# Block 0's product 4 one level deeper, its result added in memory by accumulating transfers

## The chip, the cores and the metric

One core of one Trainium2 chip. The metric is device time in microseconds of one execution, as the median of several runs. The runs of one kernel on one chip spread over 0.3 to 1.7 us, mostly under 1.1, and the median of the same kernel moves by up to 0.8 us between chips, so times are compared below between kernels that ran in turn on the same chip. (Profiles of different runs are also laid side by side; their chips can differ.)

## The reference

```python
x: (16, 512, 768)  w1: (768, 3072)  b1: (3072,)  w2: (3072, 768)      # float32

def reference(x, w1, b1, w2):
    y = np.matmul(x, w1) + b1
    y = 0.5 * y * (1.0 + erf(y / np.sqrt(2.0)))       # exact GELU
    return np.matmul(y, w2).astype(np.float32)
```

The 8192 rows are worked in eight blocks of 1024. Both products are done by Strassen-Winograd: seven products of half-size operands in place of eight. In the second product of blocks 2 to 7, each of the seven is split once more in the same way ("nested level"). Blocks 0 and 1 are mixed: most of their second product runs one level deep in row units, a few of the seven products run nested.

## The kernel before

What the change and the argument touch. A row unit of block 0 or 1 takes 128 rows and runs the products with 384 columns on the moving side; `mm` skips the products that a nested level does for it:

```python
class Unit2:                       # one-level unit: 128 rows, N2 = 384 columns, NH = 12 chunks
    def mm(self, p, dst, first, c0, c1):
        if p == 2 or self.lean and p in (1, 4):      # lean: block 1
            return
        ...
        for c in range(c0, c1):
            nc.tensor.matmul(out=dst[:, 0:N2], lhsT=a, rhs=w[:, :, c, :], ...)

    def left_done(self, row, bank):
        if row == 0:
            if not self.lean:                        # partial sum of block 0 kept for product 2
                nc.scalar.copy(out=self.rows(par02), in_=bank[:, 0:N2])
            return
        ...
```

A nested level does one of the seven products for all four row units at once, by seven sub-products of 6 chunks and 2 row halves, 192 columns each:

```python
HYBRID = ((0, 2), (1, 1), (1, 4), (1, 2))            # (block, product)

class UnitH(Unit3):
    def mm(self, q, dst, first, c0, c1):
        for c in range(NQ):                          # NQ = 6
            for t in range(2):
                nc.tensor.matmul(out=dst[:, t * N4:(t + 1) * N4], lhsT=a,     # N4 = 192
                                 rhs=self.w[q][:, c, :], ...)
    def finish(self):
        if self.p == 2:
            for n in range(NU):
                nc.gpsimd.dma_start(out=orr[...], in_=self.dst[:, n // 2, n % 2])
```

Everything is software-pipelined in periods: the matmuls of one unit are interleaved with those of the unit before, and between them "slots" put vector work and transfers in their queues. The very end of the kernel matters later: the last product of block 7 is finished in two halves, and its results leave by a few last stores:

```python
def last(self, banks):
    for t in range(2):
        self.mm(4, banks[t], True, 0, self.C, (t,))
        o = self.dst[:, 1, t, 0, :]
        tt(o, banks[t][:, t * N4:(t + 1) * N4], o, ADD)
        (nc.sync, nc.scalar)[t].dma_start(out=orr[...], in_=o)      # the last stores of the kernel
```

Of the kernel before, what the change touches and what calls it, by code (L numbers as in the profile page):

```python
# [8 lines left out]
FP32 = mybir.dt.float32  # L9
F16 = mybir.dt.float16  # L10
P = 128
ADD = mybir.AluOpType.add
# [10 lines left out]
def kernel(  # L23
# [128 lines left out]
    tmps1 = [tmp_at(o_tmp + 4 * k * RH) for k in range(2)]  # L152
    o_stage = o_wt + 2 * N + PAR
    stage = [cut(o_stage + k * WB, WB, "p (c n) -> p c n", c=NQ)
# [6 lines left out]
    for slot, off in ((T2, o_x0), (T1, o_x0 + W2_N + 2 * GS_N), (T4, o_x1 + XT_N)):  # L161
        w2v[slot] = cut(off, W2_N, "p (h c n) -> p h c n", h=2, c=NH)
    GS = [cut(o, GS_N, "p (c r) -> p c r", c=NH)
          for o in (o_x0 + W2_N, o_x0 + W2_N + GS_N, o_x1, o_x1 + GS_N)]
    osbs = [[cut(o, n).bitcast(FP32) for o, n in zip(oo, (2 * N2, 2 * N))]
            for oo in ((o_x1 + 2 * GS_N + 2 * N + 2 * N2, o_wt),
                       (o_x1 + 2 * GS_N + 2 * N, o_x1 + 2 * GS_N))]
    assert 2 * N + 4 * N2 <= PAR
    par02, par1, par4 = [cut(o, PAR).bitcast(FP32).rearrange(
        "p (r t h n) -> p r t h n", r=2, t=2, h=2) for o in (o_wt + 2 * N, 2 * XT_N, o_x1 + 2 * GS_N)]  # L170
    par11 = cut(o_w2, W2P).bitcast(FP32).rearrange("p (c n) -> p c n", c=NH)[:, 0:8, 0:N4].rearrange(
# [7 lines left out]
    def wb_at(off):  # L179
        return cut(off, WB, "p (c n) -> p c n", c=NQ)  # L180

    hyb_lev = [[strip(0, 0, 0, 0), strip(1, 1, 0, 0), Gs[0][1][:, 0:NQ, 0, 2 * P:RH], strip(1, 1, NQ, 0)],
               [strip(0, 1, 0, 0), strip(0, 0, NQ, 0), strip(0, 1, NQ, 0), strip(0, 0, 0, 2 * P)],
               [strip(0, 1, 0, 2 * P), strip(0, 0, NQ, 2 * P), strip(0, 1, NQ, 2 * P), strip(0, 0, 0, 0)],
               [strip(0, 1, 0, 0), strip(0, 0, NQ, 0), strip(0, 1, NQ, 0), strip(0, 0, NQ, 2 * P)]]
    spare = stage + [wb_at(2 * XT_N + o) for o in
                     (PAR, PAR + WB, XT_N, XT_N + WB)]
    xh_mid = [cut(2 * XT_N + XT_N + 2 * WB + k * K, K) for k in (2, 3, 4, 0, 1)]
    assert XT_N + 2 * WB + 5 * K == GR // 2
    hyb_w = {2: {7: stage[0], 5: stage[1], 6: stage[2], 4: stage[5]},  # L190
             1: dict(zip((7, 4, 5, 6), map(wb_at, (o_x0 + W2_N, o_x0 + W2_N + WB, o_x1, o_x1 + WB)))),
             4: {7: wb_at(o_x1), 4: wb_at(o_x1 + WB), 5: stage[3], 6: stage[4]}}

# [9 lines left out]
    with tc.manual_schedule():  # L203
# [63 lines left out]

        def split_w2(p, t, q=None):

            b11, b12, b21, b22 = quarters(p)  # L270

            def put(q, src, eng=nc.sync):
                eng.dma_start(out=w2s[p, q][:], in_=src)

            t = {n: spare[k] for n, k in zip((7, 5, 6, 4), t)}
            for n, a, b in ((7, b22, b12), (5, b12, b11), (6, b22, t[5]), (4, b21, t[6])):
                def f(n=n, a=a, b=b):
                    tt(t[n], a, b, SUB)
                    puts.append([LAG[0], lambda eng: put(n, t[n], eng)])
                later(WB, f, slow if q is None else q)  # L280

        def load_w2s(p, qs):
            for q in qs:
                nc.sync.dma_start(out=hyb_w[p][q], in_=w2s[p, q][:])

# [72 lines left out]

        HYBRID = ((0, 2), (1, 1), (1, 4), (1, 2))

        def operand(sb, p):
            return OPERAND[p] if sb else Gs[0][1][:, :, 0, :]

# [71 lines left out]
        class Unit2:  # L435
# [4 lines left out]
            def __init__(self, g, sb, u):  # L440
                self.g, self.sb, self.u = g, sb, u
                self.lean = sb > 0
                self.eng = nc.gpsimd if self.lean else nc.sync
                self.o = osbs1[u - NU] if self.lean else osbs[u % 2]

            def mm(self, p, dst, first, c0, c1):
                if p == 2 or self.lean and p in (1, 4):
                    return
                r = slice(self.u * P, (self.u + 1) * P)
                G1, G2 = g_of(self.sb)  # L450
                w = w2v[SLOT[p]]
                for c in range(c0, c1):
                    a = {1: G1[:, c, 0, r], 4: G2[:, c, 1, r],
                         3: GS[3][:, c, :], 5: GS[0][:, c, :], 6: GS[1][:, c, :],
                         7: GS[2][:, c, :]}[p]
                    nc.tensor.matmul(out=dst[:, 0:N2], lhsT=a, rhs=w[:, :, c, :],  # L456
                                     start=first and c == 0, stop=c == self.C - 1,
                                     skip_group_check=True)
# [7 lines left out]
            def c12(self):  # L466
                return self.o[0]

# [3 lines left out]
            def right_done(self):  # L472
                self.eng.dma_start(out=orr[:, self.sb * 8 + self.u, N2:N], in_=self.o[0])

            def left_done(self, row, bank):
                if row == 0:
                    if not self.lean:
                        nc.scalar.copy(out=self.rows(par02), in_=bank[:, 0:N2])
                    return
                if self.lean:  # L480
                    tt(self.o[1][:, 0:N2], bank[:, 0:N2], self.rows(par4), ADD)
                else:
                    nc.scalar.copy(out=self.o[1][:, 0:N2], in_=bank[:, 0:N2])
                self.eng.dma_start(out=orr[:, self.sb * 8 + NU + self.u, :], in_=self.o[1])

# [97 lines left out]
        class UnitH(Unit3):  # L583

            def __init__(self, g, sb, m):
                self.g, (self.sb, self.p) = g, HYBRID[m]
                self.lev, self.w = hyb_lev[m], dict(hyb_w[self.p])
                b11, _, b21, b22 = quarters(self.p)
                self.w.update({1: b11, 2: b21, 3: b22})
                self.add = {0: par02, 1: par1}[self.sb] if self.p == 2 else None  # L590
                self.dst = {1: par1, 4: par4, 2: par11}[self.p] if self.sb else par02
                self.alloc = lambda: None
# [15 lines left out]
            def finish(self):  # L608
                if self.p == 2:
                    for n in range(NU):  # L610
                        nc.gpsimd.dma_start(
                            out=orr[:, self.sb * 8 + n, 0:N2].rearrange("p (h n) -> p h n", h=2),
                            in_=self.dst[:, n // 2, n % 2])

# [332 lines left out]

        def drain(slot, eng=nc.sync, wait=True):
            for f in puts:
                f[0] -= 1  # L950
            while puts and not (wait and puts[0][0] > 0):
                puts.pop(0)[1](eng)
            if slot > 1:
                for f in raws[:2]:
                    f()
                del raws[:2]

        def fill_mm2_one(sb, U, slot):
            if slot == 1:
                flush(queue)  # L960
                g_sum(2, U, q=soon)
                if U == 0:
                    g_sum(3, U, q=soon)
                flush(soon)
                if U == 0:
                    for p in (1, 2, 3, 5, 6, 7, 4):
                        raw_w2(p)
                    for p, t in ((6, (0, 1, 2, 3)), (1, (4, 5, 0, 1)), (4, (2, 3, 4, 5)), (2, (0, 1, 2, 5))):
                        split_w2(p, t)
            drain(slot)  # L970
            if slot == 2:
# [10 lines left out]
            if U + 1 == NU and slot == 4:  # L982
                lev_sums(None, m=0, ks=(2,))
            if U + 1 == NU and slot == 2:
                lev_sums(None, m=1, ks=(0, 1, 2))
            if slot > 1:
# [9 lines left out]
        def fill_hyb(sb, m, slot):  # L996
            drain(slot)
            if m == 0 and slot == 1:
                load_w2s(1, (7, 4))
                lev_sums(None, m=1, ks=(3,))  # L1000
            if m == 0 and slot == 4:
                load_w2s(1, (5, 6))
            if m == 0 and slot == 5:
                lev_sums(None, m=2)
            if m == 1 and slot == 5:
                lev_sums(None, m=3, ks=(0, 1))
            if m == 1 and slot == 6:
                split_w2(7, (6, 7, 8, 9))
                split_w2(5, (6, 7, 8, 9))
            if (m, slot) in ((1, 6), (2, 1), (2, 3), (2, 5), (3, 1), (3, 5)):  # L1010
                slow.pop(0)[1]()
            if m == 2 and slot == 1:
                load_w2s(4, (7, 4))
                lev_sums(None, m=3, ks=(2,))
            if m == 2 and slot == 5:
                lev_sums(None, m=3, ks=(3,))
            if m == 3 and slot == 2:
                for k in (0, 1):
                    g_sum(k, NU)
            if slot > 0:  # L1020
                sums(1200)
            if slot == 6:
                flush(queue)
                if m == 1:
                    load_next_x(2, range(5))
                if m == 3:
                    for t in range(3):
# [5 lines left out]
        def fill_lean(sb, k, slot):  # L1033
# [12 lines left out]
            if k == 0 and slot == 4:  # L1046
                LAG[0] = 3
                split_w2(3, (1, 2, 3, 4))
            if slot > 1:
# [114 lines left out]
```

## Time and profile before

| | before |
|---|---|
| time, median of 6 runs | 852.17 us (851.51 to 852.36) |
| span in the profile | 850.3 us |
| tensor engine (PE) busy | 843.9 us |
| its instructions in the program | 12949 |
| block 0's second product, first matmul to block 2's first | 120.53 to 224.33 us |
| start of the last matmul to the end of the span ("tail") | 4.03 us |

PE is the bound: the lines in the prediction below show it. Three more lines of the PE timeline of the kernel before give the marks that I compare with later: the first matmul of the stage, the first of block 2, and the last group of the kernel. Columns: start in us, duration, engine, line, what it writes and reads, form, count.

```profile
120.53 2.11 PE L456 MATMUL bX<-arena 128*128 128x384 f16 x12
...
224.33 0.81 PE L411 MATMUL bX<-arena 128*128 128x512 f16 x3
...
845.40 1.15 PE L516 MATMUL bX<-arena 128*128 128x192 f16 x12
```

Next, from the page of the kernel before: the queue that carries refills of an instruction stream (count, MB), and the bytes to and from HBM.

```profile
q8 instruction: 50, 0.82, 0.4%
...
HBM read 182.07 MB, written 47.87 MB: 270 GB/s over the span
```

And the transfers of the last 6.1 us (844.3 to 850.4 us) of the kernel before. The GB/s row has 40 slices of 0.15 us. Below it are the last stores, with size and us from issue to landing.

```profile
GB/s 393 373 302 353 413 373 353 373 393 342 322 353 403 358 297 327 302 272 287 373 383 363 342 413 383 282 327 303 327 172 0 0 0 0 0 0 0 0 0 0
...
out_dram<-arena SPq DMA_DIRECT2D x1, 384.0 KB, 2.5
out_dram<-arena SPq DMA_DIRECT2D x1, 192.0 KB, 2.4
out_dram<-arena SPq DMA_DIRECT2D x1, 96.0 KB, 2.3
out_dram<-arena ACTq DMA_DIRECT2D x1, 96.0 KB, 2.3
```

The last stores land 2.3 to 2.5 us after their issue, and the data runs at full rate to the end. No refill of PE's stream falls in this window.

### The profile page before, as it was taken

The numbers are of one execution on the slowest core, as the hardware profiler recorded it, in microseconds if no ns is written. First come the engines' busy times: TensorE is split into PE (matmuls) and PEld (weight loads), VectorE is DVE, ScalarE is ACT, GpSimd is POOL, SyncE is SP. The second block draws the span as 40 slices with busy tenths as digits, with TensorE's granted clock in tenths as the row PEclk, the third lists the DMA queues.
The fourth block names the chain that finished last, engine by engine and source line by source line (L and its number), as shares of the span: only waits on it lengthen the run. The fifth ranks groups of instructions, "written<-read, shape, count | busy, mean of one in ns | idle before, by whom it ended". The sixth has DMA issues, their size and how long they took to land.

```text
span 850.3 us, 16583 instructions
## 1 busy us (share of the span) xinstructions
PE 843.9 (99%) x6468; PEld 571.3 (67%) x6468; DVE 671.1 (79%) x1132; ACT 423.6 (50%) x692; POOL 89.9 (11%) x147
## 2 busy tenths in 40 slices
PE   8999999999999999999999999999999999999998
PEld 5444445697544897449964499645995469944798
DVE  5766679877757998679976799667996689956998
ACT  4777762221277413773147822587216771277611
POOL 5021100022200002000020000200002100010000
PEclk9999999999999999999999999999999999999999
DMA  9998697679899699977999689995999949984398
GB/s 226 193 281 182 159 194 256 232 203 262 314 278 207 199 336 363 307 166 246 337 372 283 134 287 335 373 286 112 314 345 349 293 102 331 354 312 170 101 303 290
DMA packets 144066, 220.82 MB, mean 260 GB/s; under 512 B 61916, under 2 KB 84884, under 8 KB 143988
## 3 DMA queue, kind: packets, MB, share of 16 engines
q1 hardware_dynamic: 117536, 178.36, 67.0%
q0 software_dynamic: 26272, 41.30, 21.7%
q8 instruction: 50, 0.82, 0.4%
q14 instruction: 28, 0.23, 0.1%
q10 hardware_dynamic: 180, 0.11, 0.0%
HBM read 182.07 MB, written 47.87 MB: 270 GB/s over the span
## 4 chain that ended last, share of the span: by engine, by line
PE 98%; DMA 1%; ACT 0%; DVE 0%; SPq 0%; issue 0%; ACTq 0%
PE bY L411 21%; PE bY L516 15%; PE bX L411 14%; PE bX L516 10%; PE bW L411 7%; PE bZ L411 7%; PE bZ L516 5%; PE bW L516 5%; PE bY L456 5%; PE bZ L456 2%; PE bW L456 2%; PE bY L603 1%; PE bX L603 1%; PE bX L456 1%; DMA arena<-in_x_dram 1%; PE bX L778 0%
## 5 line engine op out<-in xcount | busy, mean ns | idle before, releaser
L208 DVE TENSOR_TENSOR arena<-arena 128x1536 f16<-128x1536 f16 (+6 forms) x634 | 405.9, 671 | 6.6 <-PE bW L456 1.0
L411 PEld LDWEIGHTS <-arena 128*128 128x128 f16 x1974 | 192.5, 98 | 224.3 <-issue 0.6
L516 PEld LDWEIGHTS <-arena 128*128 128x128 f16 x3528 | 292.1, 98 | 8.3 <-issue 0.4
L411 PE MATMUL bY<-arena 128*128 128x512 f16 x846 | 214.4, 379 | 0.1
L629 DVE TENSOR_TENSOR arena<-bY,arena 128x512 f32<-128x512 f32 (+1 forms) x102 | 69.4, 680 | 119.0 <-PE bY L411 91.9
L516 PE MATMUL bY<-arena 128*128 128x192 f16 x1500 | 138.3, 246 | 0.0
L411 PE MATMUL bX<-arena 128*128 128x512 f16 x564 | 138.2, 379 | 0.0
L622 ACT COPY bY<-bX 128x512 f32<-128x512 f32 (+1 forms) x144 | 79.1, 549 | 118.2 <-DVE arena L565 81.5
L427 ACT ACTIVATE arena<-arena,b1t 128x1024 f16<-128x1024 f32 x94 | 108.0, 1149 | 52.0 <-DVE arena L657 52.0
L642 ACT COPY arena<-bW 128x512 f32<-128x512 f32 (+1 forms) x148 | 81.5, 551 | 92.2 <-PE bW L516 44.3
L516 PE MATMUL bX<-arena 128*128 128x192 f16 x1020 | 93.1, 246 | 0.1
L657 DVE TENSOR_TENSOR arena<-bZ,arena 128x512 f32<-128x512 f32 (+1 forms) x102 | 69.2, 679 | 22.1 <-PE bZ L411 18.2
L411 PE MATMUL bZ<-arena 128*128 128x512 f16 x282 | 76.2, 379 | 0.0
L411 PE MATMUL bW<-arena 128*128 128x512 f16 x282 | 76.2, 379 | 0.0
L548 POOL DMA_DIRECT2D out_dram<-arena x42 | 30.5, 728 | 409.1 <-DVE arena L653 375.0
L432 ACT ACTIVATE arena<-bX,b1t 128x512 f16<-128x512 f32 x94 | 64.0, 681 | 10.5 <-PE bX L411 10.5
L673 ACT COPY bZ<-bY 128x512 f32<-128x512 f32 (+1 forms) x58 | 30.8, 532 | 75.6 <-PE bY L456 30.0
L456 PEld LDWEIGHTS <-arena 128*128 128x128 f16 x480 | 46.9, 98 | 31.0 <-issue 0.2
L432 ACT ACTIVATE arena<-bY,b1t 128x512 f16<-128x512 f32 x94 | 63.4, 674 | 0.0
L516 PE MATMUL bZ<-arena 128*128 128x192 f16 x504 | 48.5, 246 | 0.0
L516 PE MATMUL bW<-arena 128*128 128x192 f16 x504 | 48.4, 246 | 0.0
L316 POOL DMA_DIRECT2D arena<-in_x_dram x60 | 32.3, 546 | 152.3 <-DMA arena<-arena 142.0
(62 smaller groups left out, 413.9 us busy)
## 6 DMA issues: line engine op xcount, KB each, us to landing
arena<-w2s SPq DMA_DIRECT2D x300, 288.0 KB, 4.6
arena<-w1s SPq DMA_DIRECT2D x72, 672.0 KB, 7.0
out_dram<-arena POOLq DMA_DIRECT2D x46, 384.0 KB, 7.4
w2s<-arena SPq DMA_DIRECT2D x49, 288.0 KB, 4.1
arena<-in_x_dram POOLq DMA_DIRECT2D x60, 192.0 KB, 7.3
w1s<-arena SPq DMA_DIRECT2D x12, 672.0 KB, 6.1
arena<-in_w_dram POOLq DMA_DIRECT2D x17, 384.0 KB, 7.5
out_dram<-arena SPq DMA_DIRECT2D x9, 384.0 KB, 2.6
```

The lines of the kernel that those rows point to most:

```text
L208: nc.vector.tensor_tensor(out=o, in0=a, in1=b, op=op)
L316: nc.gpsimd.dma_start(out=xhs[t], in_=xr[:, sb * 8 + t, :])
L411: nc.tensor.matmul(out=dst[:, 0:RH], lhsT=w1_op(self.wt, slot)[:, c, :], rhs=a[:, c, :], start=first and c == 0, stop=c == self.C - 1, ski ...
L427: nc.scalar.activation(out=self.G[1][:, hi, :, :], in_=self.tmp, func=GELU, bias=b1t[:, 2 * hi + 1:2 * hi + 2])
L432: nc.scalar.activation(out=self.G[0][:, hi, row, :], in_=bank[:, 0:RH], func=GELU, bias=b1t[:, 2 * hi:2 * hi + 1])
L456: nc.tensor.matmul(out=dst[:, 0:N2], lhsT=a, rhs=w[:, :, c, :], start=first and c == 0, stop=c == self.C - 1, skip_group_check=True)
L516: nc.tensor.matmul(out=dst[:, t * N4:(t + 1) * N4], lhsT=a, rhs=w[:, c, :], start=first and c == 0 and t == ts[0], stop=c == NQ - 1, skip_ ...
L622: nc.scalar.copy(out=bY[u.g % 2][:, 0:u.F], in_=bX[u.g % 2][:, 0:u.F])
L629: nc.vector.tensor_tensor(out=u.c22(), in0=bY[u.g % 2][:, 0:u.F], in1=w[:, 0:u.F], op=ADD)
L642: nc.scalar.copy(out=w[:, 0:u.F], in_=bW[:, 0:u.F])
L657: nc.vector.tensor_tensor(out=u.c12(), in0=bZ[:, 0:u.F], in1=w[:, 0:u.F], op=ADD)
L673: nc.scalar.copy(out=bZ[:, 0:u.F], in_=bY[u.g % 2][:, 0:u.F])
```

## The change

The intent is to do block 0's product 4 by a nested level too, which needs an eighth fewer columns. Its result and product 2's can't be held back for the row units any longer, so the units store their sums without these products, and both nested results are added to the output in memory by accumulating transfers. Places in the on-chip buffers move to make room, block 1's product 1 comes after its product 4, and raw W2 stores are queued sooner.

```diff
-        HYBRID = ((0, 2), (1, 1), (1, 4), (1, 2))
+        HYBRID = ((0, 2), (0, 4), (1, 4), (1, 1), (1, 2))
@@ Unit2
-                if p == 2 or self.lean and p in (1, 4):
+                if p in (2, 4) or self.lean and p == 1:
                     return
@@ Unit2: whole rows are stored, without products 2 and 4
             def right_done(self):
-                self.eng.dma_start(out=orr[:, self.sb * 8 + self.u, N2:N], in_=self.o[0])
+                nc.gpsimd.dma_start(out=orr[..., N2:N], in_=self.o[0]) if self.lean else \
+                    nc.sync.dma_start(out=orr[:, self.sb * 8 + self.u, :], in_=self.o[0])
             def left_done(self, row, bank):
-                if row == 0:
-                    if not self.lean:
-                        nc.scalar.copy(out=self.rows(par02), in_=bank[:, 0:N2])
+                if self.lean and row == 0:
                     return
@@ UnitH
-                self.add = {0: par02, 1: par1}[self.sb] if self.p == 2 else None
+                self.add = par1 if self.sb and self.p == 2 else None
             def finish(self):
-                if self.p == 2:
-                    for n in range(NU):
-                        nc.gpsimd.dma_start(out=orr[...], in_=self.dst[:, n // 2, n % 2])
+                if self.sb and self.p != 2:
+                    return
+                for n in range(NU):
+                    o = orr[:, self.sb * 8 + self.p // 4 * NU + n, 0:N2].rearrange(...)
+                    d = self.dst[:, n // 2, n % 2]
+                    if self.sb:
+                        nc.gpsimd.dma_start(out=o, in_=d)
+                    else:
+                        nc.gpsimd.dma_start(out=o, in_=d, accum_op=ADD)
@@ raw W2 stores
-            if slot > 1:
-                for f in raws[:2]:
-                    f()
-                del raws[:2]
+            for f in raws[:n]:
+                f()
+            del raws[:n]
-            drain(slot)
+            drain(slot, 3 if U == 0 and slot > 1 else int(U + 1 == NU))
@@ ... places in the buffers, order of sums, splits and loads: cut
```

## The prediction

> **What bounds the kernel now.** I read the page's busy table first, then the tensor engine's own waits, then its instructions in order of time through block 0's second product, and only then the other engines and the transfers in that stretch. From the page, the busy table and the granted clock:
>
> ```profile
> span 850.3 us, 16583 instructions
> PE 843.9 (99%) x6468; PEld 571.3 (67%) x6468; DVE 671.1 (79%) x1132; ACT 423.6 (50%) x692; POOL 89.9 (11%) x147
> ...
> PEclk9999999999999999999999999999999999999999
> ```
>
> The tensor engine (PE) is busy for all but 6.4 us of the span, at full clock. What it waited for, in the whole run:
>
> ```profile
> PE bX L756 <- DVE arena L742: 1.2, 1, 1.2
> PE bT L330 <- DVE arena L762: 1.1, 2, 0.9
> ```
>
> Both are in the prologue. So in the stretch that the change touches no wait lies on the path; the time there is the number of matmuls times their pitch. Busy share alone would not show that (ends of matmuls are modelled), so I read pitch from starts. The timeline of PE, two places of block 0's second product: start, duration, line, target, form, count.
>
> ```profile
> 143.93 2.11 PE L456 MATMUL bW<-arena 128*128 128x384 f16 x12
> 145.88 2.11 PE L456 MATMUL bZ<-arena 128*128 128x384 f16 x12
> 147.83 4.06 PE L456 MATMUL bY<-arena 128*128 128x384 f16 x24
> ...
> 174.23 1.15 PE L603 MATMUL bY<-arena 128*128 128x192 f16 x12
> 175.22 1.15 PE L603 MATMUL bW<-arena 128*128 128x192 f16 x12
> 176.21 1.15 PE L603 MATMUL bZ<-arena 128*128 128x192 f16 x12
> ```
>
> Line 456 is the one-level unit (128 rows, moving side 384 wide), line 603 the nested level (192 wide). Twelve wide matmuls start 1.95 us after the twelve before them (143.93 to 145.88): 162.5 ns each. Twelve narrow ones take 0.99 us (174.23 to 175.22): 82.5 ns each. So one narrow matmul is half the width for slightly more than half the time. The last view, busy time by stage (PE, PEld, DVE, ACT, POOL, then clock, DMA share, GB/s), for the one-level units, the first nested period, the other nested periods:
>
> ```profile
> 120.53:163.43 42.90, 42.90 (x263) 25.54 (x262) 38.57 (x53) 10.64 (x22) 0.00 (x0) 1.00 0.74 257
> 163.43:172.25 8.82, 8.82 (x74) 6.49 (x73) 4.28 (x7) 1.80 (x4) 0.00 (x0) 1.00 0.45 143
> 172.25:193.04 20.79, 20.79 (x254) 20.79 (x253) 15.48 (x23) 5.67 (x12) 4.87 (x9) 1.00 0.84 223
> ```
>
> The vector engine (DVE) is 90% busy in the first (38.57 of 42.90 us), so it is the engine nearest to becoming the next bound.
>
> **What the Trainium skill says.** (1) "TensorE: Matmul & The Clock Gate", Back-to-back issue gap: the warm gap is width / 2.4 plus about 2.5 ns. That gives 162.5 ns at 384 and 82.5 ns at 192; this trace has exactly these. The fixed 2.5 ns is paid per matmul, so splitting costs. (2) "DMA: Bandwidth & Descriptors", SWDGE vs HWDGE vs iDMA: an accumulating transfer has to be issued from GpSimd; the change does so, and nothing in this trace accumulates yet. (3) The same page, Rules for kernel authors: an accumulate reads its destination and writes it later with nothing holding the bytes between, so the plain store before it must have landed. Here that is a wait on the GpSimd queue. (4) "Collectives: The Full Stack", The bandwidth ceiling: an add in a transfer is slower because it needs two source reads, not because of the add. No run here shows it; I use it only to double a landing time below.
>
> **The change, part by part.**
> *Product 4 in PE.* Removed: 4 row units x 12 matmuls of 384 = 48 x 162.5 ns = 7.80 us. Added: one nested level, 7 sub-products x 6 chunks x 2 row halves = 84 matmuls of 192 = 84 x 82.5 ns = 6.93 us. Net -0.87 us. PE has no wait there, so all of it lies on the path. (In columns it is 18432 against 16128, an eighth less, 0.96 us at full clock; the 36 additional matmuls give 36 x 2.5 ns = 0.09 us back.)
>
> *DVE.* Added: four operand sums 128x1536 for the new level at about 0.87 us = 3.5 us; two adds of 128x384 at 0.56 us for its right quarters = 1.1 us. Removed: the product-2 level of block 0 no longer adds the stored partial, so four adds of 0.56 us (lines 646, 670 and twice 565 between 168 and 180 us) = 2.2 us become copies on ACT. Net +2.4 us on DVE, off the path as long as operands arrive in time. By stage it is kinder than the sum: the one-level stage shrinks by three products of 1.95 us, to about 37.1 us, but four weight splits (0.75 us each) and the three sums for the second level (2.6 us) leave it, so DVE there has about 33.0 us of work in 37.1 us, 89%, as now.
>
> *ACT.* The second nested level and the row copies are a handful of 0.46 to 0.48 us copies on an engine with 10.64 us in 42.90. Free.
>
> *Transfers.* Today block 0's output is stored once, 3.1 MB, the partial sum of product 1 waiting on chip. After the change 8 stores of 384 KB write all of it, and 8 accumulating transfers of 192 KB add products 2 and 4 in memory. That is 1.6 MB more written and 1.6 MB read back, about 10 us of DMA time at 300 GB/s, in a stretch whose DMA share is 0.45 to 1.1. PE reads none of it. The raw W2 stores come 15 in the first unit instead of 10: this fills a hole, since the DMA share in 126 to 134 us is only 0.11 while the store queue waits for DVE. Product 2's split weights were on chip for both blocks before too (the six loads of split weights in this stage belong to products 1 and 4), so I count nothing for that. Loads of split weights fall from six blocks to five.
>
> *Order.* Five nested periods instead of four; block 1's product 1 now comes after product 4, since its output lies over block 0's right half, which the new level still reads. PE's order costs nothing.
>
> Sum: 852.03 - 0.87 = 851.16; I say 851.2 us.
>
> **The rivals.** First: *a wait takes back the gain.* The tightest new chain I find: two split-weight blocks of block 1's product 1 go where the first nested result lay, so their load must wait until the accumulating transfers of that result have landed. How today's stores of a nested result and today's split-weight loads fare, from the two lines' own views:
>
> ```profile
> DMA to landing us min/median/max: 2.7/4.7/6.4
> ```
> ```profile
> DMA to landing us min/median/max: 2.8/3.0/3.3
> ```
>
> The first is the result stores, the second the weight loads. Count from the start of the second nested period (173.24 now). The last of four result stores issues about 8.3 us later (the second pair starts at 180.49 and takes 1.07 us). The weights are wanted three periods of 6.93 plus one product of 0.99 later, at 21.8 us. With today's slowest landing: 8.3 + 6.4 + 3.3 = 18.0, spare 3.8 us. With the median doubled for the second read: 8.3 + 9.4 + 3.0 = 20.7, spare 1.1 us. With the slowest doubled: 8.3 + 12.8 + 3.3 = 24.4, a stall of 2.6 us. I give a stall one chance in four; it would make the time 852 to 855 us. Second: *DVE becomes the bound.* Each one-level period falls from 11.7 to 9.75 us. In the second, DVE has four sums (3.5), two evictions (1.1) and six splits (4.5) = 9.1 us, and the vector engine already runs late there: it starts an eviction at 134.29 us whose matmuls ended near 132.4. Against it: these operands are queued more than half a period ahead, and the later units have three or fewer splits. Likewise the last lean unit of block 1 gets three splits more (2.2 us), against idle DVE time of 0.46 + 1.38 us before its evictions. Each at most 1 us on PE, one chance in ten. Third: *more than predicted.* A gain beyond 0.9 us would need a hidden PE wait to go; the views show none. Fourth: the new traffic delays the weights of block 2. The stage ends at 224 us with those loads already queued and no PE wait on any load anywhere; unlikely.
>
> **Range and chances.** The runs before spread 0.6 us and another chip may shift a few tenths; no stall gives 850.6 to 851.6. With a quarter for a stall of a few us I take 850.4 to 852.8 for 8 in 10. Two per cent is 17 us, twenty times the gain and several times any stall named: faster 0.01, same 0.98, slower 0.01.
>
> **What would show it right or wrong.** Right: 48 fewer wide and 84 more narrow matmuls at unchanged pitches; the one-level units' periods 9.75 us; five nested periods of about 6.93 us; block 2's first matmul about 0.87 us earlier than at 224.33; PE's waits still only the two of the prologue. Stall theory: a PE wait in the fourth or fifth nested period, put down to a load of split weights, with the accumulating transfers landing later than about 10 us. DVE theory: a PE wait on an operand sum in the second one-level unit, or on an eviction at block 2's first unit. Wrong altogether: a time above 853 without any PE wait, or pitches that differ.

## The result, and the profile after

The changed kernel took 852.45 us in the median (852.09 to 852.74, 6 runs), beside 852.17 us for the kernel before. The ratio is 1.0004, with a 95% interval of 0.9991 to 1.0017. (A ratio is the mean time of one kernel's fast runs over that of the other's from the same rounds, so not quite the ratio of the medians.) The time is inside my range. But it is 1.25 us above my 851.2, and in the wrong direction: 0.3 us more, not 0.9 us less. I had worked the gain out exactly and it did not arrive. Where did it go?

First, what PE waited for in the whole run of the changed kernel:

```profile
PE bX L764 <- DVE arena L750: 1.2, 1, 1.2
PE bT L333 <- DVE arena L770: 0.7, 1, 0.7
PE bT L333 <- ACT arena L335: 0.4, 1, 0.4
```

All of it is in the prologue. So no wait in the stage took the gain back. Next the same three marks of the PE timeline as before:

```profile
120.25 2.11 PE L457 MATMUL bX<-arena 128*128 128x384 f16 x12
...
223.18 0.81 PE L414 MATMUL bX<-arena 128*128 128x512 f16 x3
...
844.12 1.15 PE L518 MATMUL bX<-arena 128*128 128x192 f16 x12
```

The stage took 223.18 - 120.25 = 102.93 us, against 224.33 - 120.53 = 103.80: 0.87 us less, to the hundredth what I had summed. And the last group of the kernel starts at 844.12 instead of 845.40: PE is done 1.28 us earlier. (Besides the 0.87 us, 0.28 us were there when the stage began, and 0.13 us came after it.) Yet the span is 850.5 us, 0.2 us longer. So everything is lost after PE's last matmul: from its start (0.91 us into the group) to the end of the span (the "tail") it was 4.03 us, and is 5.50 us now.

The page of the changed kernel and its transfers in the last 7.6 us (843 to 850.6 us, slices of 0.19 us):

```profile
q8 instruction: 51, 0.84, 0.4%
...
HBM read 181.78 MB, written 49.45 MB: 272 GB/s over the span
```

```profile
GB/s 372 356 340 404 348 348 458 356 315 356 327 303 303 315 150 8 16 24 259 372 360 380 352 336 372 296 323 101 24 24 20 8 0 0 0 0 0 0 0 0
...
q8 instruction: 1, 0.02, 1.0%
out_dram<-arena SPq DMA_DIRECT2D x1, 384.0 KB, 4.1
out_dram<-arena SPq DMA_DIRECT2D x1, 192.0 KB, 4.0
out_dram<-arena ACTq DMA_DIRECT2D x1, 96.0 KB, 3.5
out_dram<-arena SPq DMA_DIRECT2D x1, 96.0 KB, 3.4
```

There is one packet of the instruction queue in this window, the 51st of 51; it runs from 844.30 to 845.54 us. The data rate has a hole (150, 8, 16, 24 GB/s) and then a tail of 20 to 24 GB/s, about a sixteenth of the 350 to 380 before it. That looks like one of the 16 DMA engines finishing alone; a packet's engine is not recorded, so this is a reading. The last stores land 3.4 to 4.1 us after issue instead of 2.3 to 2.5, and one issue itself took longer. This store of 192 KB in the timeline of the store queue, before and after:

```profile
846.18 0.37 SPq L548 DMA_DIRECT2D out_dram<-arena  x1
```

```profile
844.90 1.04 SPq L550 DMA_DIRECT2D out_dram<-arena  x1
```

The Trainium skill has what is needed to see why, on a page that I had not opened: "Runtime: NRT & Kernel Launch", Instruction fetch mechanics, says that an engine's instructions are refilled in blocks of 16 KiB, that is 256 instructions, by its own DMA queue while it executes. The trace agrees: the refills are single packets of 16384 bytes, and from the first refill to the last of the changed kernel 12760 matmuls and weight loads start, 255 for each refill. PE's 12949 instructions are 50.6 blocks and show 50 refills; the changed kernel's 13022 (36 matmuls more, each with its weight load, and one wait) are 50.9 blocks and show 51. The page adds that crossing a block is "mostly hidden". In most of the kernel it is: PE has no wait after the prologue. But here the additional refill comes just as the last stores go out.

**Theory.** The change saves 0.87 us of PE, and its 72 additional instructions (36 matmuls and their weight loads) bring one more refill, which falls on the last stores and costs 1.0 to 1.5 us. It has nothing to do with what the change computes. **Rivals.** The tail of this one profile was chance; or the change's own transfers or order lengthen it.

### The profile page after: what moved, and what is told of

Its sections match the earlier page's. It is cut to its first block, busy times and chain, and to the rows that moved or that the text cites. A ratio compares the mean times of both kernels' runs of the same rounds, so it can differ in the third digit from the quotient of the medians.

```text
span 850.5 us, 16682 instructions
## 1 busy us (share of the span) xinstructions
PE 842.8 (99%) x6504; PEld 573.4 (67%) x6504; DVE 673.3 (79%) x1134; ACT 426.3 (50%) x700; POOL 94.8 (11%) x151
## 4 chain that ended last, share of the span: by engine, by line
PE 98%; DMA 1%; ACT 0%; DVE 0%; SPq 0%; issue 0%
PE bY L414 21%; PE bY L518 15%; PE bX L414 14%; PE bX L518 10%; PE bW L414 7%; PE bZ L414 7%; PE bZ L518 5%; PE bW L518 5%; PE bY L457 4%; PE bZ L457 2%; PE bW L457 2%; PE bY L606 2%; PE bX L606 1%; PE bX L457 1%; DMA arena<-in_x_dram 1%; PE bZ L606 1%
## 5 line engine op out<-in xcount | busy, mean ns | idle before, releaser
L210 DVE TENSOR_TENSOR arena<-arena 128x1536 f16<-128x1536 f16 (+6 forms) x638 | 410.1, 674 | 5.7 <-ACT arena L335 0.9
```

The costliest lines, as they stand in the source:

```text
L210: nc.vector.tensor_tensor(out=o, in0=a, in1=b, op=op)
```

## The experiments

The table has all runs. "Before" is the kernel before on the same chip. "Refill" is how long before the start of the last matmul the last refill of PE's stream began; "tail" runs from that start to the end of the span, both from the run's profile.

| kernel | PE instr. | us | before, us | ratio (95%) | refill, us | tail, us |
|---|---|---|---|---|---|---|
| before | 12949 | 852.17 | | | 8.05 | 4.03 |
| changed | 13022 | 852.45 | 852.17 | 1.0004 (0.9991-1.0017) | 0.73 | 5.50 |
| e1 changed, again | 13022 | 851.98 | 852.26 | 0.9998 (0.9985-1.0010) | 0.74 | 5.05 |
| e2 before + 36 tiny | 13021 | 853.87 | 852.26 | 1.0018 (1.0004-1.0031) | 0.57 | 5.18 |
| e3 before + 46 tiny | 13041 | 854.43 | 852.26 | 1.0025 (1.0013-1.0038) | 0.32 | 5.39 |
| e4 changed + 46 tiny | 13114 | 851.76 | 852.26 | 0.9995 (0.9982-1.0007) | 5.71 | 4.09 |
| e5 changed, again | 13022 | 852.78 | 851.97 | 1.0011 (0.9998-1.0024) | 0.50 | 5.33 |
| e6 before, 36 halved | 13021 | 853.48 | 851.97 | 1.0019 (1.0007-1.0032) | 0.40 | 5.37 |
| e7 changed, 46 halved | 13114 | 851.00 | 851.97 | 0.9989 (0.9977-1.0002) | 5.72 | 4.09 |
| e8 changed, 12 halved | 13046 | 852.49 | 851.97 | 1.0008 (0.9994-1.0022) | 0.73 | 5.36 |
| e9 as e7 | 13114 | 851.04 | 851.96 | 0.9990 (0.9977-1.0002) | 5.20 | 4.10 |
| e10 e9, slow raw stores | 13114 | 851.04 | 851.96 | 0.9990 (0.9977-1.0002) | 5.74 | 4.11 |
| e11 e9, late load | 13114 | 860.42 | 851.96 | 1.0094 (1.0079-1.0110) | 5.94 | 4.11 |

**First group: is it the refill?** e1 is the changed kernel unaltered. (The expectations of this group that give 4.9 to 5.2 or 6.3 us count from the start of the last group of matmuls, 0.91 us before the start that the table counts from.)

> The changed kernel again, on the chip of the next three. Theory: the stage gives 0.87 us, but the tensor engine's instruction stream is 72 instructions longer and its last 16 KB refill, which the kernel before does not reach, falls between the last matmuls and the final stores and delays these by about 1.2 us; so 852.4 us, with the refill near 844 us and about 6.3 us from the start of the last group of matmuls to the end. Rival (chance placement of transfers in the tail in one profile): the tail is back at 4.9 to 5.2 us and the time at 851.2.

The tail is 5.05 us with the refill at 0.74 us before the last matmul: not chance. The time came out 0.4 us lower than my number, 0.28 us below the kernel before.

e2 takes the kernel before, without any of the change, and makes PE's stream as long as the changed kernel's by tiny matmuls in the prologue, where PE warms up:

```diff
-        spin(9)
+        spin(4)
+        for k in range(5 + 36):
+            nc.tensor.matmul(out=(bX[1], bY[1])[k % 2][:, 0:48], lhsT=zero[:, 0, 0:P],
+                             rhs=zero[:, 0, 0:48], start=True, stop=True, skip_group_check=True)
```

> The kernel before with nothing of the change, only 36 more tiny matmuls (72 instructions) in the prologue where the tensor engine waits for x, so that its stream is as long as the changed kernel's. Theory (refill in the tail): a refill near the last matmuls appears, tail about 6.3 us instead of 4.9, time 853.2 to 853.5, that is +1.0 to +1.4 us over the kernel before. Rival (the change's own stores, accumulating transfers or order cost the time): 852.1, no refill effect in the tail.

The refill appeared and the tail rose to 5.18 us. But the time rose by 1.6 us, more than the tail's 1.15, and in the profile the last matmul started at 847.21 instead of 846.31 us. Only 0.17 us of that were lost where the padding stands. The rest is a PE wait of 0.85 us that ended at 40.17 us, for a vector operation behind weights that landed at 37.6 us, 0.9 us later than in the kernel before. e3 (46 in place of 36 in the same edit) was to be its control.

> Control of the padding: the kernel before with 46 tiny matmuls more, 10 more than the run above. Theory: the refill comes 20 instructions earlier, about 0.8 us before it does with 36, and should miss most of the final stores: 852.1 to 852.6, clearly below the run with 36. Rival (padding itself costs): equal to or above the run with 36.

This failed as a control. The refill did not leave the tail (0.32 us before the last matmul, tail 5.39 us), and in the prologue PE now waited 1.4 us for a piece of x. The first refill of PE's stream comes at 12.7 us in e3, at 19.2 us in the kernel before, so it now fell between the loads of x; in e2 the second, at 33.6 us instead of 38.0, fell in the late load of weights. That a refill delayed these loads too is likely but was not tested alone. e4 is the same padding by 46 in the changed kernel.

> The changed kernel with 46 tiny matmuls more in the prologue, so that its last refill comes 92 instructions (about 3.8 us) earlier, near 840.5 us, ahead of the final stores. Theory: the tail is back at 4.9 to 5.2 us and the saving of 0.87 us shows: 851.1 to 851.4, about 1.2 us below the changed kernel. Rival (the change's own cost): 852.4 as without the padding.

The tail fell back to 4.09 us as the theory says. The time did not reach 851.1 to 851.4: 851.76, since about 1 us was lost before 16 us of the span here (last matmul at 845.89 against 844.85 us in e1). So the tail followed the refill in all four runs, but the times were blurred by a bad way of padding.

**Second group: padding that costs nothing.** A matmul of 512 columns in two halves of 256 adds two instructions and no columns; by the fixed 2.5 ns per matmul that the pitches show (162.5 ns for 384, 82.5 ns for 192), 46 of them are 0.12 us. I halved them in the last block, far from the prologue:

```diff
+        halved = []
         class Unit1:
             ...
                 for c in range(c0, c1):
-                    nc.tensor.matmul(out=dst[:, 0:RH], lhsT=w1_op(self.wt, slot)[:, c, :],
-                                     rhs=a[:, c, :], start=first and c == 0, ...)
+                    cols = [slice(0, RH)]
+                    if self.sb + 1 == nsb and c and len(halved) < 46:      # 36 in e6, 12 in e8
+                        halved.append(c)
+                        cols = [slice(0, RH // 2), slice(RH // 2, RH)]
+                    for r in cols:
+                        nc.tensor.matmul(out=dst[:, r], lhsT=w1_op(self.wt, slot)[:, c, :],
+                                         rhs=a[:, c, r], start=first and c == 0, ...)
```

e5 is the changed kernel as reference on this chip, e6 the kernel before with 36 matmuls halved.

> The changed kernel once more, as the reference on this chip for the next three. Theory as before: refill about 0.7 us before the last matmul starts, 5.0 to 5.5 us from the start of the last matmul to the end; 0.0 to 0.4 us from the kernel before.

> The kernel before with 36 matmuls of 512 columns in the last block halved: 72 instructions more, no other work, 36 x 2.5 ns = 0.09 us on the tensor engine, nothing in the prologue. Theory (refill in the tail): refill near the last matmul, 5.0 to 5.5 us from the start of the last matmul to the end instead of 4.0, so +1.1 to +1.5 us over the kernel before. Rival (the +1.6 us of the run padded by 36 came from the disturbed prologue alone): +0.1 us.

e5 took 852.78 us, 0.8 us over the kernel before; more than the 0.4 I had allowed, with the tail at 5.33 us. e6 took 853.48 us, 1.5 us over the kernel before, with an interval that leaves out 1. Nothing of the change is in e6. The transfers of its last 7.5 us (843.8 to 851.3 us):

```profile
GB/s 385 360 303 385 377 369 369 377 382 336 369 279 307 287 238 340 352 377 369 393 312 328 328 303 66 25 25 25 21 25 21 16 0 0 0 0 0 0 0 0
...
q8 instruction: 1, 0.02, 0.8%
out_dram<-arena SPq DMA_DIRECT2D x1, 384.0 KB, 3.9
...
out_dram<-arena SPq DMA_DIRECT2D x1, 96.0 KB, 3.7
out_dram<-arena ACTq DMA_DIRECT2D x1, 96.0 KB, 3.6
```

The reader sees the same signs as in the changed kernel: the refill in the window, the tail of 16 to 25 GB/s, landings of 3.6 to 4.0 us where the kernel before has 2.3 to 2.5. There is no hole in the rate this time. Of the seven profiles with a late refill, all have the slow tail; the hole is in three (changed, e1, e8), where the issue of the 192 KB store took 0.67 to 1.04 us instead of 0.37. How the refill does either stays a reading.

> The changed kernel with 46 matmuls of the last block halved: 92 instructions more, +0.12 us on the tensor engine, the last refill near 840.3 us. Theory: 4.0 to 4.2 us from the start of the last matmul to the end, and the time 0.9 us (0.7 to 1.2) below the changed kernel, 0.7 to 1.0 below the kernel before. Rival (the end is set by the change's own transfers): as the changed kernel or 0.1 us more.

e7 took 851.00 us (850.71 to 851.28), 0.97 us below the kernel before and 1.78 us below the changed kernel. The last is more than the 0.7 to 1.2 that I expected, because e5 was slower than I expected. Its last 6.1 us (843 to 849.1 us):

```profile
GB/s 353 383 332 383 373 393 353 353 383 393 302 373 393 323 302 327 302 217 343 363 363 363 393 342 388 297 307 318 322 91 0 0 0 0 0 0 0 0 0 0
...
out_dram<-arena SPq DMA_DIRECT2D x1, 384.0 KB, 2.5
out_dram<-arena SPq DMA_DIRECT2D x1, 192.0 KB, 2.3
out_dram<-arena SPq DMA_DIRECT2D x1, 96.0 KB, 2.3
out_dram<-arena ACTq DMA_DIRECT2D x1, 96.0 KB, 2.3
```

With the refill out of this window, hole, tail and late landings are gone, with all the accumulating transfers and the whole change in place. Together e6 and e7 settle it: the cost goes with the place of the refill and not with the change. (The kernel before with 46 halved matmuls, which should cost it only the 0.12 us, was not run.)

> The changed kernel with 12 matmuls of the last block halved: the refill comes 24 instructions, about 1.0 us, earlier, near 843.1 us, and should be over (0.9 to 1.2 us) before the last stores are issued. Theory: most of the tail comes back, 4.0 to 4.5 us from the start of the last matmul to the end, 0.5 to 1.0 us below the changed kernel. If a refill delayed every store of the last microseconds alike, it stays at 5 us.

e8 missed. I had counted that 24 instructions more would bring the refill 1.0 us earlier. It came 0.73 us before the last matmul, as in the changed kernel, and the tail stayed at 5.36 us. The place of the refill does not follow the count of instructions one for one: in the twelve profiles that have a 51st refill, 12957 to 13021 matmuls and weight loads had started when it began. That is a scatter of 64, more than the 24 that I had added; by what rule it arises I have not found out. So e8 says nothing on whether a refill that ends just before the last stores would be harmless.

**Third group: other steps of the prediction.** e9 repeats e7 on another chip. e10 takes the raw stores back to their old pace, e11 delays the loads that have to wait for accumulating transfers.

> The changed kernel with 46 halved matmuls again, on another chip and as the reference of the next two. Theory: it beats the kernel before by 0.7 to 1.0 us, with 4.0 to 4.2 us from the start of the last matmul to the end.

```diff
-            drain(slot, 3 if U == 0 and slot > 1 else int(U + 1 == NU))      # e10
+            drain(slot, 2 if slot > 1 else 0)

-            if m == 2 and slot == 6:                                         # e11
+            if m == 3 and slot == 6:
                 load_w2s(3, (7, 4))
```

> The same, with the raw W2 stores back at the old pace (two at a time through the first units, none held for the last). The tensor engine waits for no transfer in that stage, so: within 0.3 us of the reference. If the moved stores were worth something by themselves: 0.5 us or more slower, with a wait of the tensor engine or a late operand sum in the one-level units.

> The same, with the two last loads of block 1's product 1 weights, which have to wait for the accumulating transfers, queued one period later. The first rival of the prediction named this as the tightest new chain. If it has about 3.7 us to spare as the trace suggests, one period of 6.93 us later turns into a wait of the tensor engine of 1 to 3 us on a load, and as much more time; the wait would begin near 186.9 us.

e9: 851.04 us, 0.92 us below the kernel before. The stated interval just reaches 1 in both e7 and e9, but on neither chip does any of the five runs overlap with the nine runs of the kernel before. e10: 851.04 us too; moving the raw stores is worth nothing measurable. e11: 860.42 us (4 runs), 9.4 us more than e9. PE's wait, and its timeline around it:

```profile
PE bY L613 <- DMA arena<-w2s: 7.7, 1, 7.7
```

```profile
184.49 2.14 PE L613 MATMUL bX<-arena 128*128 128x192 f16 x24
194.33 2.10 PE L613 MATMUL bY<-arena 128*128 128x192 f16 x12 [7.70 <-DMA arena<-w2s]
196.22 1.00 PE L613 MATMUL bW<-arena 128*128 128x192 f16 x5
```

The last link of the chain, from the loads to PE, is real, and the wait begins where I had said, but I was wrong by far on the size (1 to 3 us expected). Queued one period later, the loads stand behind four stores of split weights, which wait for the vector engine; the first was issued at 186.39 us, they took up to 7.9 us to land (at most 5.4 in the changed kernel), and PE went on at 194.33. So the queue held these loads, and not the accumulating transfers: how long the latter can hold a load e11 does not test. Nor is the wait all of it: the next twelve matmuls take 1.89 us instead of 0.99, and the granted clock, 1.00 before the wait, was 0.54 between 194.3 and 200.4 us.

## Why the prediction was right or wrong

**The term for PE was right.** The stage became 0.87 us shorter, as 48 x 162.5 ns against 84 x 82.5 ns says. The one-level periods are 9.75 us (128.05, 137.80, 147.55, 157.30 us), the nested ones 6.93 us (171.10, 178.03, 184.96 us), at unchanged pitches. (The page on the tensor engine that the prediction cites gives its formula for an isolated matmul; for a stream of weight loads and matmuls it has other spacings, about 131 ns for 512 columns. This trace is such a stream and keeps to the formula: six of 512 columns take 1.30 us, 216 ns each.)

**The step that failed is the sum**, "852.03 - 0.87 = 851.16", and under it the claim "PE has no wait there, so all of it lies on the path". It holds for the path up to PE's last matmul. The sum took the rest of the span for constant. It is not: the same 36 additional matmuls that I charged 0.09 us on PE made PE's stream longer by 72 instructions and brought a refill into the last stores. The missing term is +1.0 to +1.5 us: tails of 5.05 to 5.50 us in the seven profiles with the refill near the last matmul, 4.03 to 4.11 us in the six without. With it the sum is 852.03 - 0.87 + 1.0 to 1.5 = 852.2 to 852.7, and the median was 852.45. It is met only to about half a microsecond: from the kernel before, the changed one differed by +0.28, -0.28 (e1) and +0.81 us (e5), where the sum says +0.1 to +0.6. That the range held the time was luck, for a reason that I had not thought of: I had widened it upward for a stall in the stage, and there was none. Without the refill (e7, e9) the gain is 0.97 and 0.92 us, which is the mechanism that I had described, though these kernels also carry 0.12 us of halved matmuls. That would leave 0.75 us; I can't account for the other 0.2, which is within what the same kernel moves between runs.

**First rival, a wait on the accumulating transfers: the chain was found, and it has time to spare.** Their landing, and that of the split-weight loads, in the changed kernel (each from its own line's view):

```profile
DMA to landing us min/median/max: 4.1/6.0/8.8
```

```profile
DMA to landing us min/median/max: 3.1/4.5/5.4
```

I had doubled 4.7 us to 9.4; the median became 6.0, 1.3 times. Even that need not be the add: the four plain stores of block 1's nested result took 6.2 us in the median in the same trace, so the traffic around them may be all of it. The doubling that I took from the skill's "Collectives: The Full Stack" (which says of ReduceScatter that its add needs two source reads) did not show in a landing; no run isolates the cost of the add. What I had not foreseen is the issue: 1254 ns each on GpSimd, against 645 ns for the plain store before and 725 ns for the plain one in the same trace. The last loads in the chain are issued by 178.1 us and land by 183.5 at the slowest; PE wants them at 186.9, so some 3 us are spare. e11 shows how expensive a late load is.

**Second rival, the vector engine as the bound: no.** For the one-level units, the first of the three stretches of the prediction (PE, PEld, DVE, ACT, POOL, clock, DMA share, GB/s):

```profile
120.25:157.30 37.05, 37.05 (x227) 22.02 (x226) 32.79 (x46) 10.02 (x21) 0.00 (x0) 1.00 0.73 251
```

32.79 us in 37.05, 89%: I had worked out 33.0 in 37.1. DVE's total rose from 671.1 to 673.3 us, by 2.2 where I had 2.4.

**Transfers.** Written bytes rose by 1.58 MB, as I said (1.6). The 1.6 MB read back don't appear in the page's figure for reads, which fell by 0.29 MB, one split-weight load of 288 KB. That the raw stores "fill a hole" is true (the DMA share from 126 to 134 us rose from 0.11 to 0.56), and irrelevant, as e10 shows.

**Third rival, "a gain beyond 0.9 us would need a hidden PE wait".** This was the wrong question. The hidden time was not in PE's waits at all, but after PE's end.

## What to carry to other kernels

When one engine is busy for 99% of the span, the change in its work gives the change in the time only if the head and the tail of the span stay as they are; compare the last matmul's start and the tail separately, since a gain and a loss of 1 us each look like nothing. Unrolled kernels fetch their own instructions by DMA: before a change that adds or removes instructions, see how far the last refill is from the last stores, and afterwards see whether it moved. If it fell into them, extra instructions can move it away: here 46 halved matmuls did, for a tenth of a microsecond, and 12 did not. Do it far from a prologue that is waiting for its own loads.

## What the Trainium skill lacked or had wrong

- "Runtime: NRT & Kernel Launch", Instruction fetch mechanics: it calls the cost of crossing a 16 KiB block mostly hidden. It lacks what a refill can cost the kernel's own transfers: with one of 0.9 to 1.2 us near the last matmul, the last stores of the changed kernel landed 3.4 to 4.1 us after issue instead of 2.3 to 2.5, and over all profiles the tail was 5.05 to 5.50 us against 4.03 to 4.11.
- The same page gives 256 instructions per block; the distance between refills agrees (255 matmuls and weight loads). It lacks when a refill is called for: 24 instructions more did not move it from 0.73 us before the last matmul (e8), 92 more moved it to 5.2 to 5.9 us (e4, e7, e9 to e11).
- "CRC Debugging", Comparing the Two Runs, names queue 14 for refills; here the 16 KiB refills that follow PE's stream are on queue 8, and queue 14 carries packets of 8 KiB. Its 28 packets (0.23 MB) are about what the 3642 instructions of the other four engines in the program before come to at 64 bytes each, so it may carry their refills; no run shows it.
- "DMA: Bandwidth & Descriptors" has no time for an accumulating transfer to HBM: 192 KB in fp32, 1536 bytes per row, took 6.0 us in the median from issue to landing and 1254 ns to issue, against 4.7 us and 645 ns for the plain store of the same size in the kernel before, and 6.2 us and 725 ns for the plain one in the changed kernel.
